# Routed experts on one core: the expert with the fewest tokens takes the last turn

## The chip, the cores and the metric

One NeuronCore of a Trainium2 chip runs the whole program in one launch. The metric is the device time of one execution in microseconds (us); lower is better. Times of the kernel before are the median of three runs; everything about single instructions comes from one profiled execution.

## What is computed

Two layers of a hybrid block over 256 tokens of width 1024. The first layer ends in a dense feed-forward part, the second in eight routed experts, and the change touches the experts alone. Cut to them:

```python
logits = xf @ router                              # [256, 8]
top_val, top_idx = lax.top_k(logits, 2)           # two experts for each token
gates = softmax(top_val)
for e in range(8):                                # over the tokens that chose e
    y_e = (silu(x_e @ w_gate[e]) * (x_e @ w_up[e])) @ w_down[e]
    out[token] += gate * y_e
```

All is float32. An expert has three matrices of 1024 x 3584, 44 MB together. A token can choose any two experts, so the numbers of tokens differ; for this input the experts 0 to 7 have 58, 77, 58, 62, 58, 73, 50 and 76 of them.

## The kernel before

**Order of the work.** The experts come last in the program, after two mixers and the dense feed-forward part. They run one after another, 0 to 7, in `run_experts` (L1714). The weights of an expert are cut into 42 units of 1 MB (`expert_units`, L1376): for each of the chunks in `WIDE` (three of 1024 hidden columns, one of 512) the units of the gate matrix, then those of the up matrix, and one chunk behind them those of the down matrix. All 336 units of the eight experts are one list in the order of their use.

**The feed.** `Feed` (L1398) holds a ring of 18 tiles. The first 18 units are loaded before the experts begin (`load_one`, L1414 is its transfer). After that `send` (L1408 is its transfer) puts the next unit of the list into the ring as soon as the matmuls that read the unit 18 places earlier are done. All these transfers are issued by one engine, SP, in program order, into one queue. `done(k)` in `expert` is k calls of `send`.

**Router.** DVE forms `sel` (which experts a token chose), `pos` (a token's place in its expert, 4096 or more where it didn't choose it) and `gate`. PE sums the counts into `cps`. `count` (L1485) makes `cnt`, then `levi`: 2 for an expert with up to 64 tokens, 1 for up to 96, 0 for more. `gates` (L1353) needs an exponential of ACT and writes `gate`.

**An expert.** `entry(e)` multiplies the first 64 tokens by the 8 units of the first chunk (four of gate, four of up). Then each of PE, ACT, DVE and SP loads `levi[e]` into a register (L1727) and branches (L1787) into one of three versions, the arms of a `tc.Switch`: n = 2, 1 or 0 extra pieces of 32 tokens beyond the first 64. The arm `expert(e, n, ...)` holds the rest: with n > 0 it gathers the extra tokens (`gather(e, 1, AUX)`), adds the results of the expert before to `h` (`scatter`), runs the chunks (`half` for the first 64 tokens, `rest` for the extra ones; `down`, `down_rest`), and the sends of that stretch. Near its end it gathers the next expert's first 64 tokens (`gather(e + 1, 0, ...)`). With n > 0 it closes with `scatter_rest`, or after the last expert with `scatter_last`, followed by the final norm and the output. The hint for the register, the load and the branch of SP stand in front of the sends of the arm.

**Names in the rows.** `mb` and `mc` are PSUM banks (gate and up products; down products, transposes, gathers), `ring` a weight unit, `xT` the gathered tokens, `mh` the hidden values, `ge` the one-hot matrix of a gather, `ys` an expert's result. L97 is the helper for accumulating matmuls, L94 for the others, L100 for transposes.

Of the kernel before, what the change touches and what calls it, by code (L numbers as in the profile page):

```python
# [12 lines left out]
I32 = mybir.dt.int32  # L13
AF = mybir.ActivationFunctionType
OP = mybir.AluOpType
AX = mybir.AxisListType
PSUM = bass.MemoryType.PSUM

P = 128
D = 1024  # L20
# [5 lines left out]
NE = 8  # L26
# [9 lines left out]
def kernel(  # L36
# [37 lines left out]
    nc = tc.nc  # L74
    act = nc.scalar.activation
    vec = nc.vector
# [10 lines left out]
    def mm_bank(name):  # L87
        return pp["mm"].tile([P, 512], F32, tag="mm", name=name)
# [16 lines left out]
    def stream(name, elems, order, side, units, lead, each=None):  # L105
# [6 lines left out]
        def open_raw(stack, once={}, spare=()):  # L112
            pools = [stack.enter_context(tc.tile_pool(name=f"raw{name}{g}", bufs=1, side=side, reuse_waits="tile"))
                     for g in range(n_raw - len(spare))] + list(spare)
            slots.extend([(pools[g], f"raw{g}") for g in order if g not in once])
            for g in order:
                if g in once and units:
                    load_one(*once[g])
                else:
                    load(1 + sum(r[4] for r in raw))  # L120
# [11 lines left out]
        def load(limit=n_raw):  # L132
            while slots and units and sum(r[4] for r in raw) < limit:
                load_one(*slots[0], 1)
                slots.append(slots.pop(0))
# [30 lines left out]
        def get():  # L166
# [3 lines left out]
            return u  # L170

        S.open_raw, S.open_split, S.load_one, S.feed = open_raw, open_split, load_one, units.extend
        S.split, S.ahead, S.get, S.load, S.spl = split, ahead, get, load, spl
        return S
# [93 lines left out]
    iota_f = cst.tile([P, P], F32, name="iota_f")  # L268
# [116 lines left out]
    class Norm:  # L385
        def __init__(self, name):
            self.name, self.ss, self.rstd, self.dg, self.bank = name, {}, {}, {}, None
# [988 lines left out]
    def expert_units():  # L1376
        units = []

        def gate_up(e, c, w):
            for src in (moe_w_gate[0, e], moe_w_up[0, e]):  # L1380
                for k in range(0, KT, 4 // w):
                    units.append((src[k * P:(k + 4 // w) * P, c * 512:(c + w) * 512]
                                  .rearrange("(k p) n -> p k n", p=P), (4 // w, 512 * w)))

        def down(e, c, w):
            for j in range(0, 4 * w, 2):
                r0 = c * 512 + j * P
                units.append((moe_w_down[0, e][r0:r0 + 2 * P, :].rearrange("(p k) n -> p k n", p=P), (2, D)))

        for e in range(NE):  # L1390
            for i, cw in enumerate(WIDE):
                gate_up(e, *cw)
                if i:
                    down(e, *WIDE[i - 1])
            down(e, *WIDE[-1])
        return units

    class Feed:  # L1398
        def __init__(self, units):
            self.units, self.ring, self.sent, self.used = units, [], 0, 0  # L1400

        def view(self, u):
            a, b = self.units[u][1]
            return self.ring[u % len(self.ring)][:, : a * b].rearrange("p (a b) -> p a b", a=a)

        def send(self):
            if self.sent < len(self.units):
                nc.sync.dma_start(self.view(self.sent), self.units[self.sent][0])  # L1408
                self.sent += 1

        def load_one(self, pool, tag):
            self.ring.append(pool.tile([P, 2048], F32, tag=tag, name=f"ring{len(self.ring)}"))
            a, b = self.units[self.sent][1]
            nc.sync.dma_start(self.ring[-1][:, : a * b].rearrange("p (a b) -> p a b", a=a), self.units[self.sent][0])  # L1414
            self.sent += 1

        def get(self, n):
# [6 lines left out]
    def moe(W, R, pend, tidy, prep):  # L1424
# [31 lines left out]
        def make_hn(q, half):  # L1456
            ns = slice(half * 512, (half + 1) * 512)
            vec.scalar_tensor_tensor(hn[:, q, ns], h[:, q, ns], rstd[q], g2b[:, ns], op0=OP.mult, op1=OP.mult)
# [14 lines left out]
        pick(1)  # L1473
        places(lambda: make_hn(1, 0))
        pos = R.t["pos"]
        cnt = R.small("cnt", [P, NE])
        lev = R.small("lev", [P, NE])
        levi = R.small("levi", [P, NE], I32)
        cmax = R.small("cmax", [P, 1])
        cmaxi = R.small("cmaxi", [P, 1], I32)  # L1480
        cps = mm_bank("cps")
# [1 line left out]
            mm(cps[:, :NE], prep[1], R.t["sel"][:, q, :], q == 0, q == 1)  # L1483

        def count():  # L1485
            vec.tensor_copy(cnt, cps[:, :NE])
            vec.tensor_scalar(lev, cnt, 64.5, None, op0=OP.is_lt)
            vec.scalar_tensor_tensor(lev, cnt, 96.5, lev, op0=OP.is_lt, op1=OP.add)
            vec.tensor_copy(levi, lev)
            vec.tensor_reduce(cmax, cnt, axis=AX.X, op=OP.max)  # L1490
            vec.tensor_copy(cmaxi, cmax)

        ge = m2.tile([P, 4, 2, P], F32, name="ge")
# [8 lines left out]
        def onehot(e, base, vs=range(4)):  # L1502
            for v in vs:
                for q in range(2):
                    vec.tensor_scalar(ge[:, v, q, :], slot[:, v, :], float(base), pos[:, q, e:e + 1],  # L1505
                                      op0=OP.add, op1=OP.is_equal)
# [15 lines left out]
        def gather(e, b, bank):  # L1522
            for k in range(KT):
                for q in range(2):
                    mm(bank[:, 64 * k:64 * k + 64], hn[:, q, k * P:(k + 1) * P], ge[:, 0, q, 64 * b:64 * b + 64], q == 0, q == 1)
            act(X[e % 2][:, :, 64 * b:64 * b + 64], bank.rearrange("p (k t) -> p k t", k=KT), AF.Copy)
# [89 lines left out]
        def result():  # L1616
            o = SL, Hid
            ns = [slice(512 * m, 512 * m + 512) for m in range(2)]
            for q in range(2):
                vec.scalar_tensor_tensor(msz[:, q:q + 1], ssz[:, q, 0:1], RMS_EPS, ssz[:, q, 1:2], op0=OP.add, op1=OP.add)  # L1620
                nc.gpsimd.tensor_tensor(rz[:, q:q + 1], msz[:, q:q + 1], mhalf[:, 0:1], op=OP.pow)  # L1621
                vec.tensor_tensor(o[q][1], h[:, q, ns[1]], fg[:, ns[1]], op=OP.mult)
            for q in range(2):
                vec.scalar_tensor_tensor(o[q][0], h[:, q, ns[0]], rz[:, q:q + 1], fg[:, ns[0]], op0=OP.mult, op1=OP.mult)
                act(o[q][1], o[q][1], AF.Copy, scale=rz[:, q:q + 1])
                nc.sync.dma_start(out[0, q * P:(q + 1) * P, ns[0]], o[q][0])
                nc.scalar.dma_start(out[0, q * P:(q + 1) * P, ns[1]], o[q][1])
# [20 lines left out]
        def entry(e):  # L1648
            x = X[e % 2]
            w = WIDE[0][1]  # L1650
            first = []
            for i in range(2):
                first.append(units(2 * w))
                half(GU[i], x, first[i])
                if i == 0:
                    silu(w, 0, 256)
            return first
# [56 lines left out]
        def run_experts(base):  # L1714
            onehot(0, base, range(1))
            if base == 0:
                make_hn(1, 1)
            gather(0, 0, AUX)
            if base == 0:
                count()  # L1720
                gates()
            onehot(0, base, range(1, 4))
            for e in range(NE):
                if base:
                    expert(e, 2, base, entry(e))
                    continue
                lv = nc.values_load(levi[0:1, e:e + 1], engines=ENG, min_val=0, max_val=2)  # L1727
                tc.switch_hint({g: lv for g in ENG}, 3, f"ex{e}")
                first = entry(e)
                at = W.used, W.sent  # L1730
                for arm in tc.Switch({g: lv for g in ENG}, 3, hint=f"ex{e}"):
                    W.used, W.sent = at
                    expert(e, 2 - arm, base, first)
            if base == 0:
                nc.sync.dma_start(fg, final_g.partition_broadcast(P))
            result()

        run_experts(0)
        rv = nc.values_load(cmaxi[0:1, 0:1], min_val=0, max_val=T)
        with tc.If(rv > P):  # L1740
# [15 lines left out]
    W, pend, tidy = mixer(0, Norm("a0"), None, Nf, ffn_weights)  # L1756
# [3 lines left out]
    R = Route()  # L1760
    W, pend, tidy = mixer(1, Na, pend, R, lambda: Feed(expert_units()))
    mst.close()
    moe(W, R, pend, tidy, prep)

_INS = ['x', 'norm1_g', 'w_in', 'pool_w', 'pool_scale', 'conv_w', 'conv_b', 'conv_ln_g', 'conv_ln_b', 'shift_mu', 'rwkv_w0', 'rwkv_w2', 'rwkv_a0', 'rwkv_a2', 'rwkv_g2', 'rwkv_k_k', 'rwkv_k_a', 'rwkv_r_k', 'rwkv_gn_g', 'rwkv_gn_b', 'rwkv_v0', 'rwkv_v1', 'rwkv_v2', 'w_out', 'norm2_g', 'ffn_w_gate', 'ffn_w_up', 'ffn_w_down', 'moe_router', 'moe_w_gate', 'moe_w_up', 'moe_w_down', 'final_g']
# [26 lines left out]
```

## Time and profile before

| what | value |
|---|---|
| median of 3 runs (lowest, highest) | 1427.1 us (1426.35, 1427.16) |
| the profiled execution's own time | 1425.54 us |
| its span, first to last instruction | 1423.6 us |
| PE busy over the span | 1332.7 us, 94% |
| DVE, ACT, POOL busy | 495.4, 296.3, 62.4 us |
| mean granted TensorE clock | 0.991 of full speed |
| read from HBM | 419.86 MB |

The span is 1.9 us less than the profiled execution's time, and that execution is 1.6 us under the median. The experts take the span from about 540 us on. The page cuts the span into 40 slices of 35.6 us each and gives the busy tenths of each engine, the busy share of the 16 DMA engines and the rate that they moved. A share a little over 1 in a window means that all of them were moving data throughout. In a row of the timeline, the bracket at the end names the idle time before the instruction and what ended it.

### The profile page before, as it was taken

What the parts mean: (1) busy time and instruction counts of PE and PEld (TensorE: products, weight loads), DVE (VectorE), ACT (ScalarE), POOL (GpSimd) and SP (SyncE); (2) the same over time, 40 slices, a digit from 0 to 9 for tenths busy, and PEclk for the clock granted to TensorE, in tenths of its full rate; (3) what the DMA queues carried; (4) which work ended last, traced back from release to release, by engine and by line L of the source; (5) the groups of instructions that cost most, each with busy time, mean ns of one, the idle gap of its engine ahead of it and who ended that gap; (6) DMA issues with size and microseconds to landing.
All of it is one profiled execution on the core that took longest, in us unless ns stands there. A gap on an engine that the chain in (4) does not pass through costs nothing.

```text
span 1423.6 us, 32188 instructions
## 1 busy us (share of the span) xinstructions
PE 1332.7 (94%) x14243; PEld 957.1 (67%) x14243; DVE 495.4 (35%) x1065; ACT 296.3 (21%) x524; POOL 62.4 (4%) x89
## 2 busy tenths in 40 slices
PE   8999999999999899999999999888888999999996
PEld 7988799999898877557655555344346665556662
DVE  7999655555698973101010111001001110111001
ACT  6534454444653432000000000000000000000001
POOL 3020220000102010000000000000000000000000
PEclk9999999999999997999999999999999999999998
DMA  5523635551452279999999999999999998999970
GB/s 181 165 74 116 200 129 189 178 180 64 128 162 79 76 284 382 415 416 414 411 418 359 413 416 418 416 415 416 414 417 410 410 413 358 416 415 414 416 280 34
DMA packets 138329, 423.80 MB, mean 298 GB/s; under 512 B 8400, under 2 KB 51800, under 8 KB 123768
## 3 DMA queue, kind: packets, MB, share of 16 engines
q1 hardware_dynamic: 137144, 419.10, 75.7%
q8 instruction: 124, 2.03, 0.6%
q0 software_dynamic: 672, 1.31, 0.3%
q14 instruction: 101, 0.83, 0.2%
q10 hardware_dynamic: 288, 0.52, 0.1%
HBM read 419.86 MB, written 1.05 MB: 296 GB/s over the span
## 4 chain that ended last, share of the span: by engine, by line
PE 70%; DMA 16%; DVE 9%; issue 2%; ACT 1%; POOL 1%; SPq 0%; ACTq 0%; POOLq 0%; DVEq 0%
PE mb L97 26%; PE mc L97 14%; PE fps L94 8%; DMA ring<-in_moe_w_up_dram 7%; DMA ring<-in_moe_w_down_dram 5%; DMA ring<-in_moe_w_gate_dram 4%; PE fd L94 4%; DVE cy L557 3%; PE wo L94 2%; PE pjc L94 2%; PE pjr L94 2%; PE mb L94 2%; PE mc L100 1%; PE mc L94 1%; PE pjp L94 1%
## 5 line engine op out<-in xcount | busy, mean ns | idle before, releaser
L97 PE MATMUL mb<-ring,xT 128*64 128x256 f32 (+1 forms) x6272 | 490.1, 338 | 32.0 <-DMA ring<-in_moe_w_up_dram 13.0
L97 PEld LDWEIGHTS mb<-ring,xT 128*64 128x64 f32 (+1 forms) x6272 | 330.3, 125 | 190.1 <-issue 41.0
L97 PE MATMUL mc<-ring,mh 128*64 128x512 f32 (+1 forms) x1568 | 240.7, 504 | 17.6 <-DMA ring<-in_moe_w_down_dram 9.2
L97 PEld LDWEIGHTS mc<-ring,mh 128*64 128x64 f32 (+1 forms) x1568 | 82.3, 125 | 160.2 <-issue 116.6
L1566 DVE COPY mh<-mc 128x256 f32<-128x256 f32 (+1 forms) x56 | 24.3, 471 | 339.7 <-PE mc L100 339.7
L1551 ACT ACTIVATE sl<-mb 128x256 f32<-128x256 f32 (+2 forms) x62 | 22.9, 398 | 461.9 <-PE mc L100 384.4
L1556 DVE TENSOR_TENSOR sl<-sl,mb 128x256 f32<-128x256 f32 (+1 forms) x56 | 25.1, 469 | 199.0 <-PE mb L97 198.9
L1589 DVE TENSOR_TENSOR h<-h,mc 128x512 f32<-128x512 f32 x34 | 21.5, 683 | 170.5 <-PE mc L97 170.1
L94 PE MATMUL fps<-xhf,wl_fu 128*128 128x256 f32 x176 | 49.9, 284 | 0.1
L94 PE MATMUL fps<-xhf,wh_fg 128*128 128x256 f32 x176 | 49.9, 284 | 0.0
L94 PE MATMUL fps<-xlf,wh_fu 128*128 128x256 f32 x176 | 49.8, 283 | 0.0
L94 PE MATMUL fps<-xhf,wh_fu 128*128 128x256 f32 x176 | 49.8, 283 | 0.0
L94 PE MATMUL fps<-xlf,wh_fg 128*128 128x256 f32 x176 | 49.8, 283 | 0.0
L94 PE MATMUL fps<-xhf,wl_fg 128*128 128x256 f32 x176 | 49.8, 283 | 0.0
L557 DVE SCALAR_TENSOR_TENSOR cy<-cu,parC,cy 128x256 f32<-128x256 f32 x120 | 49.5, 475 | 0.0
L1621 POOL TENSOR_TENSOR rstdz<-msz,mhalf 128x1 f32<-128x1 f32 x2 | 1.6, 830 | 874.3 <-DVE msz L1620 874.3
L151 DVE TENSOR_TENSOR wl_fg<-fg,wh_fg 128x2048 fp32r<-128x2048 f32 x10 | 24.5, 2448 | 30.7 <-ACT wh_fg L147 30.7
L94 PE MATMUL fd<-wh_fd,hh 128*128 128x512 f32 x88 | 34.4, 390 | 0.0
L94 PE MATMUL fd<-wl_fd,hh 128*128 128x512 f32 x88 | 34.4, 390 | 0.0
L94 PE MATMUL fd<-wh_fd,hl 128*128 128x512 f32 x88 | 34.2, 389 | 0.0
L1505 DVE TENSOR_SCALAR ge<-slot,pos 128x128 f32<-128x128 f32 x64 | 14.1, 281 | 57.4 <-PE mc L100 57.3
L94 PEld LDWEIGHTS fps<-xhf,wh_fg 128*128 128x128 f32 x176 | 33.8, 192 | 0.3
(418 smaller groups left out, 2001.1 us busy)
## 6 DMA issues: line engine op xcount, KB each, us to landing
ring<-in_moe_w_gate_dram SPq DMA_DIRECT2D x112, 1024.0 KB
ring<-in_moe_w_up_dram SPq DMA_DIRECT2D x112, 1024.0 KB
ring<-in_moe_w_down_dram SPq DMA_DIRECT2D x112, 1024.0 KB
fg<-in_ffn_w_gate_dram SPq DMA_DIRECT2D x11, 1024.0 KB
fu<-in_ffn_w_up_dram SPq DMA_DIRECT2D x11, 1024.0 KB
fd<-in_ffn_w_down_dram SPq DMA_DIRECT2D x11, 1024.0 KB
wo<-in_w_out_dram SPq DMA_DIRECT2D x16, 512.0 KB
wik<-in_w_in_dram SPq DMA_DIRECT2D x8, 512.0 KB
```

The costliest lines, as they stand in the source:

```text
L94: nc.tensor.matmul(o, lhsT, rhs, start=start, stop=stop)
L97: nc.tensor.matmul(o, lhsT, rhs, start=start, stop=True, skip_group_check=True)
L100: nc.tensor.transpose(o, i, ident[:n, :n])
L151: vec.tensor_tensor(wl[:, :n], t[:, :n], wh.bitcast(F32)[:, :n], op=OP.subtract)
L557: vec.scalar_tensor_tensor(cy[:, i, :], src, wc, cy[:, i, :], op0=OP.mult, op1=OP.add)
L1505: vec.tensor_scalar(ge[:, v, q, :], slot[:, v, :], float(base), pos[:, q, e:e + 1], op0=OP.add, op1=OP.is_equal)
L1551: act(SL[i][:, a:b], GU[0][i][:, a:b], AF.Silu)
L1556: vec.tensor_tensor(SL[i][:, 0:b], SL[i][:, 0:b], GU[1][i][:, 0:b], op=OP.mult)
L1566: vec.tensor_copy(Hid[i][:, 0:b], o[:, 0:b])
L1589: vec.tensor_tensor(h[:, q, ns], h[:, q, ns], ps[n], op=OP.add)
L1621: nc.gpsimd.tensor_tensor(rz[:, q:q + 1], msz[:, q:q + 1], mhalf[:, 0:1], op=OP.pow)
```

## The change

A new function, `least_last`, runs on DVE before the first expert. It finds the expert with the fewest tokens among 1 to 7 and swaps its columns in the counts, in `pos` and in `gate` with those of the eighth place. A second row of `cnt` holds each place's expert number; swapped likewise and cast to integers it is `who`. `levi` is now formed for expert 0 first, and for the other seven after the swap. At the head of each turn but the last SP loads the next turn's expert number from `who` into a register, and the source address of each weight transfer of the turns 1 to 7 is formed from it. For this input the order of the experts becomes 0, 1, 2, 3, 4, 5, 7, 6.

```diff
         def gate_up(e, c, w):
-            for src in (moe_w_gate[0, e], moe_w_up[0, e]):
+            for src in (moe_w_gate, moe_w_up):
                 for k in range(0, KT, 4 // w):
-                    units.append((src[k * P:(k + 4 // w) * P, c * 512:(c + w) * 512]
-                                  .rearrange("(k p) n -> p k n", p=P), (4 // w, 512 * w)))
+                    units.append((lambda x, src=src, k=k: src[0, x, k * P:(k + 4 // w) * P, c * 512:(c + w) * 512]
+                                  .rearrange("(k p) n -> p k n", p=P), (4 // w, 512 * w), e))
...
+            self.index = {}
+
+        def source(self):
+            make, _, e = self.units[self.sent]
+            return make(e) if e == 0 else make(self.index[e])
...
-                nc.sync.dma_start(self.view(self.sent), self.units[self.sent][0])
+                nc.sync.dma_start(self.view(self.sent), self.source())
...
         def count():
-            vec.tensor_copy(cnt, cps[:, :NE])
-            vec.tensor_scalar(lev, cnt, 64.5, None, op0=OP.is_lt)
-            vec.scalar_tensor_tensor(lev, cnt, 96.5, lev, op0=OP.is_lt, op1=OP.add)
-            vec.tensor_copy(levi, lev)
-            vec.tensor_reduce(cmax, cnt, axis=AX.X, op=OP.max)
+            vec.tensor_copy(cnt[:, 0, :], cps[:, :NE])
+            vec.tensor_copy(cnt[:, 1, :], iota_f[:, 0:NE])
+            levels(0, 1)
+
+        def levels(a, b):
+            c = cnt[:, 0, a:b]
+            vec.tensor_scalar(lev[:, a:b], c, 64.5, None, op0=OP.is_lt)
+            vec.scalar_tensor_tensor(lev[:, a:b], c, 96.5, lev[:, a:b], op0=OP.is_lt, op1=OP.add)
+            vec.tensor_copy(levi[:, a:b], lev[:, a:b])
+
+        def least_last():
...
+            vec.scalar_tensor_tensor(score, cnt[:, 0, :], 8.0, cnt[:, 1, :], op0=OP.mult, op1=OP.add)
+            vec.tensor_reduce(least, score[:, ones_], axis=AX.X, op=OP.min)
+            vec.tensor_scalar(took[:, ones_], score[:, ones_], least, None, op0=OP.is_equal)
+            vec.tensor_scalar(kept[:, ones_], took[:, ones_], 0.0, None, op0=OP.is_equal)
...
+            for v in (cnt, pos, R.t["gate"]):
+                w = v[:, :, ones_]
+                x = spare[:, :, ones_]
+                vec.tensor_tensor(x, w, tb, op=OP.mult)
+                vec.tensor_reduce(last, x, axis=AX.X, op=OP.add)
+                vec.tensor_tensor(x, v[:, :, NE - 1:NE].to_broadcast(b3), tb, op=OP.mult)
+                vec.tensor_tensor(w, w, kb, op=OP.mult)
+                vec.tensor_tensor(w, w, x, op=OP.add)
+                vec.tensor_copy(v[:, :, NE - 1], last)
+            levels(1, NE)
+            vec.tensor_copy(who, cnt[:, 1, :])
+            vec.tensor_reduce(cmax, cnt[:, 0, :], axis=AX.X, op=OP.max)
             vec.tensor_copy(cmaxi, cmax)
...
             onehot(0, base, range(1, 4))
+            if base == 0:
+                least_last()
             for e in range(NE):
+                if e + 1 < NE:
+                    W.index[e + 1] = nc.values_load(who[0:1, e + 1:e + 2], engines=(mybir.EngineType.SP,), min_val=1, max_val=NE - 1)
                 if base:
```

How the instructions stand now, at the three places of which the prediction speaks. The first is SP between the last of the 18 preloaded units and the first sends of the first expert. Before:

```order
L1414 DMA ring_6861<-in_moe_w_down_dram 128x2048 [waits DVE_49,DMAHW0_49,PE_49,Activation_49]
L1727 TENSOR_LOAD levi [waits DVE_49]
L1727 ISA x2
L1728 SWITCH_STRIDE
L1728 ISA
L1728 BRANCH_PREFETCH_HINT
L1787 SWITCH_STRIDE
L1787 ISA x2
L1731 BRANCH_PREFETCH_HINT
L1408 DMA ring_5494<-in_moe_w_down_dram 128x2048 [waits DMAHW1_49,PE_49]
```

Now:

```order
L1419 DMA ring_6861<-in_moe_w_down_dram 128x2048 [waits DVE_49,DMAHW0_49,PE_49,Activation_49]
L1761 TENSOR_LOAD who [waits DVE_49]
L1761 ISA x2
L1765 TENSOR_LOAD levi
L1765 ISA x2
L1766 SWITCH_STRIDE
L1766 ISA
L1766 BRANCH_PREFETCH_HINT
L1825 SWITCH_STRIDE
L1825 ISA x2
L1769 BRANCH_PREFETCH_HINT
L1413 DMA ring_5494<-in_moe_w_down_dram 128x2048 [waits DMAHW1_49,PE_49]
```

A load of `who` with a wait for DVE has come ahead of the branch, and every send of the first expert stands behind it.

The second place is DVE from `gate` to its branch. Before:

```order
L1364 TENSOR_TENSOR gate<-ex,zs 128x16 [waits DVE_49]
L1505 TENSOR_SCALAR ge<-slot,pos 128x128 x6
L1727 TENSOR_LOAD levi [waits DVE_49]
L1728 SWITCH_STRIDE
L1728 ISA
```

Now 28 instructions stand between `ge` and the load; the first seven and the last five of them:

```order
L1364 TENSOR_TENSOR gate<-ex,zs 128x16 [waits DVE_49]
L1539 TENSOR_SCALAR ge<-slot,pos 128x128 x6
L1506 SCALAR_TENSOR_TENSOR score<-cnt 128x8
L1507 TENSOR_REDUCE least<-score 128x1 [waits DVE_49]
L1508 TENSOR_SCALAR took<-score,least 128x7 [waits DVE_49]
L1509 TENSOR_SCALAR kept<-took 128x7 [waits DVE_49]
L1516 TENSOR_TENSOR spare<-cnt,took 128x2x7
L1517 TENSOR_REDUCE last<-spare 128x2 [waits DVE_49]
L1518 TENSOR_TENSOR spare<-cnt,took 128x2x7 [waits DVE_49]
```

```order
L1499 SCALAR_TENSOR_TENSOR lev<-cnt,lev 128x7 [waits DVE_49]
L1500 CAST levi<-lev 128x7 [waits DVE_49]
L1523 CAST who<-cnt 128x8
L1524 TENSOR_REDUCE cmax<-cnt 128x1
L1525 CAST cmaxi<-cmax 128x1 [waits DVE_49]
L1765 TENSOR_LOAD levi [waits DVE_49]
```

`who` is the 26th of the 28, behind both the swap of `gate` and the three instructions of `levi`.

The third place is SP among the sends, where the units of the first expert end and those of the second begin. Now:

```order
L1413 DMA ring_6426<-in_moe_w_down_dram 128x2048 [waits DMAHW7_49,PE_49]
L1413 DMA ring_6428<-in_moe_w_down_dram 128x2048 [waits DMAHW0_49,PE_49]
L1413 ISA
L1413 DMA ring_6486<-in_moe_w_gate_dram 128x2x1024 [waits DMAHW1_49,PE_49]
L1413 ISA
L1413 DMA ring_6764<-in_moe_w_gate_dram 128x2x1024 [waits DMAHW2_49,PE_49]
```

From the second expert's units on, one register instruction stands before each transfer; before the change there was none.

## Rows read from the trace of the kernel before

**Rows 1.** The page: GB/s moved by DMA in 40 slices of 35.6 us.

```profile
GB/s 181 165 74 116 200 129 189 178 180 64 128 162 79 76 284 382 415 416 414 411 418 359 413 416 418 416 415 416 414 417 410 410 413 358 416 415 414 416 280 34
```

**Rows 2.** Windows: length, busy of five engines, granted clock, DMA share, GB/s.

```profile
560.00:760.00 200.00, 197.01 (x2311) 122.24 (x2309) 20.40 (x52) 9.86 (x24) 0.00 (x0) 1.00 1.02 413
760.00:768.00 8.00, 5.89 (x37) 2.82 (x38) 2.48 (x4) 0.98 (x2) 0.00 (x0) 1.00 1.00 392
768.00:776.00 8.00, 7.77 (x74) 5.36 (x72) 0.00 (x0) 0.77 (x2) 0.00 (x0) 1.00 0.60 222
...
784.00:1075.00 291.00, 254.48 (x1826) 133.43 (x1824) 30.38 (x83) 12.15 (x30) 0.00 (x0) 1.00 1.02 415
```

**Rows 3.** Timeline of PE: start us, us, instruction; the end of expert 5's `entry`.

```profile
1075.90 1.95 PE L97 MATMUL mb<-ring,xT 128*64 128x256 f32 x16 [0.65 <-DMA ring<-in_moe_w_up_dram]
1077.78 3.79 PE L94 MATMUL mc<-ge,hn 128*128 128x64 f32 x32
```

**Rows 4.** Windows as in rows 2, from expert 6's `entry` to the last `down`.

```profile
1198.00:1407.00 209.00, 205.57 (x2359) 126.90 (x2361) 20.96 (x48) 9.77 (x24) 0.00 (x0) 1.00 0.85 344
...
1270.00:1295.00 25.00, 24.04 (x191) 14.69 (x188) 0.42 (x1) 1.96 (x4) 0.00 (x0) 1.00 1.03 417
```

**Rows 5.** Timeline of DVE where `gate` is made: start us, us, instruction.

```profile
552.77 0.17 DVE L1363 RECIPROCAL zs<-zs 128x2 f32<-128x2 f32 x1
552.97 0.17 DVE L1364 TENSOR_TENSOR gate<-ex,zs 128x16 f32<-128x16 f32 x1
553.06 1.26 DVE L1505 TENSOR_SCALAR ge<-slot,pos 128x128 f32<-128x128 f32 x6
```

**Rows 6.** Timeline of SP: the first two sends of the first expert.

```profile
554.29 2.88 SPq L1408 DMA_DIRECT2D ring<-in_moe_w_down_dram  x2
```

**Rows 7.** SP's register load, branch, arm's first instruction, 540 to 560: ns, start us.

```profile
L1727 SPq TENSOR_LOAD <-levi x1: 468/468/468, 544.3 to 544.3; - x1
...
L1727 SPq SEQ_ASSERT  x1: 28/28/28, 545.1 to 545.1; - x1
...
L1787 SPq COMPARE_BRANCH  x1: 58/58/58, 545.8 to 545.8; - x1
...
L1731 SPq BRANCH_PREFETCH_HINT  x1: 36/36/36, 551.3 to 551.3; - x1
```

**Rows 8.** The same, 760 to 775; the branch into the arm is the second.

```profile
L1787 SPq COMPARE_BRANCH  x2: 43/43/43, 764.0 to 770.4; - x2
...
L1731 SPq BRANCH_PREFETCH_HINT  x1: 36/36/36, 773.0 to 773.0; - x1
```

**Rows 9.** Timeline of PE: the end of expert 5 and `entry` of expert 6.

```profile
1194.90 1.03 PE L97 MATMUL mb<-ys,gT 64*128 64x256 f32 x8
1198.04 14.03 PE L97 MATMUL mb<-ring,xT 128*64 128x256 f32 x128 [2.10 <-DMA ring<-in_moe_w_down_dram]
1212.00 1.99 PE L97 MATMUL mc<-ys,gT 64*128 64x512 f32 x8
```

**Rows 10.** Timeline of PE: expert 2 after its `entry`, to expert 3's.

```profile
782.04 1.99 PE L97 MATMUL mc<-ys,gT 64*128 64x512 f32 x8
...
842.24 3.79 PE L94 MATMUL mb<-ge,hn 128*128 128x64 f32 x32
...
850.30 6.00 PE L97 MATMUL mb<-ring,xT 128*64 128x256 f32 x54
```

**Rows 11.** Timeline of all engines after the last expert's last `down`.

```profile
1407.63 1.14 PE L97 MATMUL mc<-ys,gT 64*128 64x256 f32 x8
1407.74 0.60 ACT L1708 ACTIVATE ys<-mc 128x512 f32<-128x512 f32 x1 [3.15 <-PE mc L97]
...
1409.46 1.02 PE L97 MATMUL mc<-ys,gT 64*128 64x512 f32 x4
...
1410.52 1.29 DVE L1589 TENSOR_TENSOR h<-h,mc 128x512 f32<-128x512 f32 x2 [8.39 <-PE mc L97]
```

**Rows 12.** The chain of waits at expert 7's `entry`: start us, us, what.

```profile
1271.88 21.04 DMA ring<-in_moe_w_up_dram
```

More of the change, by code (lines that the diff above doesn't have):

```diff
@@ L1387, in down @@
                 r0 = c * 512 + j * P
-                units.append((moe_w_down[0, e][r0:r0 + 2 * P, :].rearrange("(p k) n -> p k n", p=P), (2, D)))
+                units.append((lambda x, r0=r0: moe_w_down[0, x, r0:r0 + 2 * P, :].rearrange("(p k) n -> p k n", p=P), (2, D), e))
         for e in range(NE):
@@ L1413, in load_one @@
             a, b = self.units[self.sent][1]
-            nc.sync.dma_start(self.ring[-1][:, : a * b].rearrange("p (a b) -> p a b", a=a), self.units[self.sent][0])
+            nc.sync.dma_start(self.ring[-1][:, : a * b].rearrange("p (a b) -> p a b", a=a), self.source())
             self.sent += 1
@@ L1475, in moe @@
         pos = R.t["pos"]
-        cnt = R.small("cnt", [P, NE])
+        cnt = R.small("cnt")
+        who = R.small("who", [P, NE], I32)
         lev = R.small("lev", [P, NE])
@@ L1485, in count @@
         def count():
-            vec.tensor_copy(cnt, cps[:, :NE])
-            vec.tensor_scalar(lev, cnt, 64.5, None, op0=OP.is_lt)
-            vec.scalar_tensor_tensor(lev, cnt, 96.5, lev, op0=OP.is_lt, op1=OP.add)
-            vec.tensor_copy(levi, lev)
-            vec.tensor_reduce(cmax, cnt, axis=AX.X, op=OP.max)
+            vec.tensor_copy(cnt[:, 0, :], cps[:, :NE])
[7 more added lines that the diff above has]
+        def least_last():
+            score, took, kept = [R.small(n, [P, NE]) for n in ("score", "took", "kept")]
+            least = R.small("least", [P, 1])
+            ones_ = slice(1, NE)
+            vec.scalar_tensor_tensor(score, cnt[:, 0, :], 8.0, cnt[:, 1, :], op0=OP.mult, op1=OP.add)
+            vec.tensor_reduce(least, score[:, ones_], axis=AX.X, op=OP.min)
+            vec.tensor_scalar(took[:, ones_], score[:, ones_], least, None, op0=OP.is_equal)
+            vec.tensor_scalar(kept[:, ones_], took[:, ones_], 0.0, None, op0=OP.is_equal)
+            spare, last = R.small("spare"), R.small("last", [P, 2])
+            b3 = [P, 2, NE - 1]
+            tb, kb = [t[:, None, ones_].to_broadcast(b3) for t in (took, kept)]
+            for v in (cnt, pos, R.t["gate"]):
[10 more added lines that the diff above has]
+            vec.tensor_reduce(cmax, cnt[:, 0, :], axis=AX.X, op=OP.max)
             vec.tensor_copy(cmaxi, cmax)
```

## Prediction

> **What bounds the kernel now.** I read the page's slices first, then windows by stage, then the timelines where one stage hands over to the next. In the slices the transfers run at 410 to 418 GB/s for nearly the whole of the experts, with two lower slices, 359 and 358, and they stop in the last but one [rows 1]. The windows say which side waits. From 784 to 1075 us the DMA share is 1.02 and PE is busy for 254 of 291 us: the transfers bound that stretch [rows 2]. It ends in the `entry` of expert 5, where each unit's 16 matmuls still wait 0.65 us for a transfer; the work on its extra tokens follows at 1077.8 without a wait [rows 3]. From 1198 on PE is the bound: 205.6 of 209 us busy, against a DMA share of 0.85 [rows 4]. So the end of the program has two parts. Up to about 1078 it is as late as the stream of weights; after that it is as late as the sum of PE's work.
>
> Two facts follow. A delay of the stream anywhere before 1075 moves the end, unless a hole in the stream takes it up. And once PE is never idle, the order of the experts changes the end only by what each order adds to or takes from PE's work.
>
> **The swap.** For this input the last turns become expert 7 (76 tokens, one extra piece) and then expert 6 (50 tokens, none). I add PE's time from the start of the seventh turn's `entry`, 1198.04.
> - A turn with one extra piece: the `entry` takes 14.0 us (1198.04 to 1212.00) [rows 9]; from the gather of the extra tokens to the next `entry`, closing included, 120.3 us (1077.78 to 1198.04) [rows 3, 9]. Sum 134.3.
> - A turn without one: `entry` 14.0, the rest 68.3 (782.04 to 850.30), of which 3.8 are the gather for a next expert [rows 10]. As the last turn 14.0 + 68.3 - 3.8 = 78.5.
> - Together 212.8 us. Before, the same stretch took 1407.6 - 1198.0 = 209.6 us [rows 9, 11]. That is 3.2 us more. The price is the closing of an expert with extra tokens: the scattering matmuls and a gap of 2.10 us ahead of the next `entry` [rows 9]. Experts 1 and 5 pay it before; expert 7, being last, has its own closing. Now it pays as well.
> - The end gets shorter. Before, DVE's first addition starts 2.9 us after the last `down` (1407.6 to 1410.5). Without the extra pieces' 16 matmuls there remain ACT's copy, 0.6 us from 0.1 us after the last `down`, and four matmuls of 1.0 us: 1.8 us [rows 11]. That is 1.1 us less.
>
> The swap costs 3.2 - 1.1 = **2.1 us**. I see no gain from having little left to do after the last transfer, since PE arrives there late in either order. The transfers stay ahead in the last turn: 24 units are to be issued after its `entry` begins, 2.53 us each (1.05 MB at 415 GB/s), 61 us, plus a pause of SP of some 9 us at the change of arms [rows 1, 8]. That makes 70 us, and PE needs the last unit about 76 us after the `entry` begins.
>
> **The wait at the start.** This is the larger term. SP now loads `who` ahead of its first branch, and all sends of the first expert stand behind that, though they need no index.
> - DVE: the six instructions on `ge` end at 554.3. `who` is the 26th instruction after them. An instruction that waits for the one before it starts 0.20 us later, one that doesn't 0.09 [rows 5]; 20 of the 26 wait: 20 x 0.20 + 6 x 0.09 = 4.5 us, so `who` is there at about 558.9. All at 0.09 it would be 556.7, all at 0.20 559.5.
> - SP: from a load to the step behind its check 0.8 us; from the load of `levi` to the branch 1.5 us [rows 7]. The branch comes at 558.9 + 0.8 + 1.5 = 561.2.
> - Branch: the arm's first instruction came 5.5 us after it in the first turn, with the transfers at full rate [rows 7], and 2.6 us after it at 770.4, with the transfers at a share of 0.60 [rows 2, 8]. Now the 18 preloaded units have landed before SP gets there, so I take 2.6 and keep 5.5 for the range. The first send then goes out at about 563.9 instead of 554.3 [rows 6]: **9.6 us** later.
>
> [...]
>
> - What takes it up: from 560 to 760 the stream is full, so nothing is regained there [rows 2]. From 760 to 776 it has a hole: 8 x (1.02 - 0.60) + 8 x (1.02 - 1.00) = 3.5 us [rows 2]. It lies where SP, after an expert with extra tokens, sends nothing between its two branches at 764.0 and 770.4 and the fetch behind them [rows 8]. A stream that is 9.6 us late still has data to move then, so the hole fills. PE's lateness in expert 1 would shift the pause too, but the hole is filled as long as that is under 6 us. After it the stream is full to 1075 again. There remain 9.6 - 3.5 = **6.1 us**, and they pass on to the `entry` of expert 5 and to all that follows.
>
> DVE's other work is not late: its next task, the product of the first chunk, waits for PE's `entry` of expert 0, 14.0 us of matmuls at least [rows 9]. PE and ACT load `levi` of expert 0, which is formed earlier as before. The later loads of `who` on SP, seven in all, and the register instruction ahead of 294 transfers cost nothing while the queue is full; at 0.8 us a turn they shorten the 6 us of lead that the transfers keep in the last turn.
>
> **Sum.** 1425.5 for the profiled execution (span 1423.6 and 1.9 around it) + 2.1 + 6.1 = 1433.7. The median of the runs lies 1.6 higher: 1427.1 + 8.2 = **1435.3 us**, slower by 0.6%. About 0.2%, 2.9 us, is what a measurement of this kernel can tell from no change.
>
> **The rivals.**
> - *Faster: PE really waits 21 us at expert 7's `entry`, and the short turn takes that out.* The chain of waits says 21.0 us of DMA there [rows 12]. If PE were idle then, a last turn that needs less PE time would let the end follow the last transfer: 1435.3 - 21 = 1414. It decides if PE's idle time there is more than 11 us. Against it: from 1270 to 1295 PE is busy for 24.0 of 25 us [rows 4]; the chain counts a transfer that ran beside PE's work. Chance 0.05.
> - *No change: the wait for `who` ends in the hole.* That needs a first send no later than 554.3 + 3.5 = 557.8. Then only the swap stays: 1429.2. For it: the first sends feed tiles that PE doesn't need for many us, and I have not seen DVE run these small instructions. Against it: even at 0.09 us each the first send would be at 561.7. Chance 0.13.
> - *Slower still: the fetch behind the branch takes 5.5 us again and the hole does not fill*, because SP's pause there grows as well: 1435.3 + 2.9 + 3.5 = 1441.7. [...] Chance 0.12.
> - *The swap does not take place* (the index stays as it was): 1427.1 + 6.1 = 1433.2. Nothing in the order of the instructions speaks for it. Chance 0.02.
>
> **How the numbers follow.** My forecast has 0.68; its own range, from `who` at 556.7 to a fetch of 5.5 us, is 1433 to 1439. With the no-change case and most of the slower one the range is 1429.0 to 1441.5. Slower by over 0.2%: 0.68 + 0.12 + 0.02 = 0.82; within: 0.13; faster: 0.05.
>
> **What would show it.** In the new profile SP's first send should stand near 564 instead of 554.3, `who` should be cast near 559, and a window around 556 to 564 should show the DMA share near zero. The slice that had 359 GB/s should be full. Expert 5's `entry` should end some 6 us later. The seventh turn should take 134 us on PE and the eighth 78.5 to its last `down`, with no wait for a transfer. I am wrong if expert 5's `entry` ends at the old time, if PE is idle for several us in the last turn, or if the end comes closer to the last transfer without the total moving.

## The result and the profile after

The changed kernel takes 1443.5 us, the median of three runs (1441.87 to 1444.83), against 1427.1. The ratio is 1.012, with a 95% interval of 1.0105 to 1.0134: slower by 16.4 us, where 8.2 were forecast and the range ended at 1441.5. The sign was right and the size forecast was half of what was measured. The profiled execution took 1441.87 us, with a span of 1440.1 and a mean granted clock of 0.991, as before.

The two terms that were forecast came about as forecast. First the start. The timeline of DVE in the changed kernel (start us, us, instruction):

```profile
552.80 0.18 DVE L1364 TENSOR_TENSOR gate<-ex,zs 128x16 f32<-128x16 f32 x1
552.89 1.26 DVE L1539 TENSOR_SCALAR ge<-slot,pos 128x128 f32<-128x128 f32 x6
554.07 0.17 DVE L1506 SCALAR_TENSOR_TENSOR score<-cnt 128x8 f32<-128x8 f32 x1
...
558.60 0.16 DVE L1523 CAST who<-cnt 128x8 int32<-128x8 f32 x1
```

SP's instructions from 554 to 565 us, line by line (ns, and in us the first and the last start):

```profile
L1761 SPq TENSOR_LOAD <-who x1: 474/474/474, 558.8 to 558.8; - x1
...
L1765 SPq TENSOR_LOAD <-levi x1: 275/275/275, 559.6 to 559.6; - x1
...
L1825 SPq COMPARE_BRANCH  x1: 63/63/63, 560.9 to 560.9; - x1
...
L1769 SPq BRANCH_PREFETCH_HINT  x1: 40/40/40, 563.6 to 563.6; - x1
```

And SP's first sends in its timeline:

```profile
563.71 1.18 SPq L1413 DMA_DIRECT2D ring<-in_moe_w_down_dram  x2
```

`who` is cast at 558.6 (forecast 558.9), SP branches at 560.9 (561.2), the arm begins 2.7 us later (2.6) and the first send goes out at 563.71 (563.9), where it stood at 554.29 [rows 6]. The windows of the changed kernel show the pause, and that the hole at 768 to 776 us is gone (columns as in rows 2):

```profile
556.00:564.00 8.00, 8.00 (x78) 5.21 (x76) 2.57 (x19) 0.77 (x2) 0.00 (x0) 1.00 0.02 7
564.00:760.00 196.00, 188.87 (x2209) 115.06 (x2205) 19.84 (x51) 8.60 (x21) 0.00 (x0) 1.00 1.02 406
760.00:768.00 8.00, 7.35 (x69) 4.08 (x68) 0.56 (x1) 0.98 (x2) 0.00 (x0) 1.00 1.03 410
768.00:776.00 8.00, 5.71 (x51) 4.13 (x49) 2.48 (x4) 0.60 (x1) 0.00 (x0) 1.00 1.04 407
784.00:1090.00 306.00, 261.28 (x1860) 135.54 (x1858) 31.11 (x84) 12.13 (x30) 0.00 (x0) 1.00 1.02 406
```

Then the swap. The timeline of PE at the seventh turn's `entry`, at the eighth's (cut off by the window at 1348), and of all engines at the last `down` and behind it:

```profile
1213.09 14.04 PE L97 MATMUL mb<-ring,xT 128*64 128x256 f32 x128 [2.27 <-issue]
...
1346.02 2.34 PE L97 MATMUL mb<-ring,xT 128*64 128x256 f32 x19 [1.21 <-DMA ring<-in_moe_w_down_dram]
...
1421.20 3.65 PE L97 MATMUL mc<-ring,mh 128*64 128x512 f32 x16 [0.52 <-DVE mh L1600]
...
1424.96 0.60 ACT L1742 ACTIVATE ys<-mc 128x512 f32<-128x512 f32 x1 [15.00 <-PE mc L97]
...
1426.77 1.28 DVE L1623 TENSOR_TENSOR h<-h,mc 128x512 f32<-128x512 f32 x2 [5.62 <-PE mc L97]
```

The seventh turn takes 132.9 us (134.3 forecast). The eighth takes 78.8 to the end of its last `down` (78.5), at 1424.85, 0.1 us ahead of ACT's copy. DVE's first addition follows 1.9 us behind it (1.8). From the seventh `entry` to the end of the span it is now 227.0 us, against 1423.6 - 1198.04 = 225.6 before [rows 9]. The swap therefore costs 1.4 us in these two executions, where the forecast was 2.1.

What was not forecast stands in the last column of the windows. At the same DMA share of 1.02 the stream moves 406 GB/s where it moved 413 and 415 [rows 2]. The slices of the page say the same, 398 to 412 in full ones where 410 to 418 stood [rows 1]:

```profile
GB/s 190 166 61 140 173 139 192 188 176 75 114 150 75 113 293 292 406 410 409 404 412 407 404 410 402 407 410 401 407 411 398 407 409 343 272 408 380 343 407 173
```

So the stream arrives much later at the place where it last decides. This is the end of expert 5's `entry` in the timeline of PE, which answers to rows 3:

```profile
1091.05 1.95 PE L97 MATMUL mb<-ring,xT 128*64 128x256 f32 x16 [0.65 <-DMA ring<-in_moe_w_up_dram]
1092.93 3.79 PE L94 MATMUL mc<-ge,hn 128*128 128x64 f32 x32
```

It was 1077.78 and is 1092.93: 15.15 us later instead of 6.1. The rest, 16.5 - 15.15 = 1.4 us of the span, is the swap.

### The profile page after: what moved, and what is told of

It reads as the page before. It is cut to its first block, busy times and chain, and to the rows that moved or that the text cites. A ratio compares the mean times of both kernels' runs of the same rounds, so it can differ in the third digit from the quotient of the medians.

```text
span 1440.1 us, 32831 instructions
## 1 busy us (share of the span) xinstructions
PE 1333.3 (93%) x14243; PEld 955.6 (66%) x14243; DVE 502.0 (35%) x1096; ACT 296.2 (21%) x524; POOL 62.8 (4%) x89
## 4 chain that ended last, share of the span: by engine, by line
PE 66%; DMA 20%; DVE 10%; issue 2%; ACT 1%; POOL 1%; SPq 0%; ACTq 0%; DVEq 0%; POOLq 0%
PE mb L97 25%; PE mc L97 13%; PE fps L94 8%; DMA ring<-in_moe_w_up_dram 8%; DMA ring<-in_moe_w_down_dram 7%; PE fd L94 4%; DMA ring<-in_moe_w_gate_dram 3%; DVE cy L557 3%; PE mb L94 2%; PE pjk L94 2%; PE pjr L94 2%; PE pjc L94 1%; PE mc L100 1%; PE mc L94 1%; PE wo L94 1%
```

## The experiments

**What the theories are.** The DMA engines were busy throughout in both kernels (a share of 1.02) and moved less, so each packet (one of the pieces in which the trace lists a transfer, here of 2048, 4096 or 8192 bytes) takes longer. From 640 to 1100 us the trace has a median of 162 ns for the packets of 4096 bytes in the changed kernel and 159 before; for 2048 bytes it is 87 and 84, for 8192 bytes 313 and 309. Three or four nanoseconds come on top whatever the size. The transfers of the first expert, whose addresses are still constants, show it too: its 4096-byte packets have a median of 162 ns where they had 159, its 2048-byte packets 87 where they had 84.

*Theory A* looks at where the packets go. The new small tiles (`who`, `score`, `took`, `kept`, `least`, `spare`, `last` and a second row of `cnt`) lie in the same pool as the old ones, and whatever is allocated behind that pool moves up by 288 bytes a partition. Among it are ring tiles 7 to 15. In the compiled programs they lie at:

```
                   ring 7, 8, ... 15 (bytes)         above a multiple of 256
before             32256, 40448, ... 97792           0
after              32544, 40736, ... 98080           32
ring 0 to 6, 16, 17, both kernels                    224
```

Theory A is that this move is what costs: a packet into a tile that begins off a multiple of 256 bytes takes three to four nanoseconds longer, whatever its size. It names no mechanism, and no run shows one. That 256 is the size that counts is an assumption of mine at this point; runs 2, 7 and 8 move the tiles by 288, 64 and 256 bytes. *Rival B* is that the addresses read from a register, or SP's extra instruction ahead of each transfer, slow the stream. The runs are compared by their ratio to the kernel before on the same chip, and by a distance within one profile: from the start of the first `entry` to the extra tokens of expert 5, 527.2 us before and 542.5 after the change. The first `entry` in PE's timeline, before and after:

```profile
550.57 15.72 PE L97 MATMUL mb<-ring,xT 128*64 128x256 f32 x120 [0.69 <-ACT xT L1526]
...
550.40 15.83 PE L97 MATMUL mb<-ring,xT 128*64 128x256 f32 x132 [0.69 <-ACT xT L1560]
```

**1. The ring put back, the rest of the change kept.**

```diff
-            spare, last = R.small("spare"), R.small("last", [P, 2])
+            spare, last = R.small("spare", [P, 2, NE + 28]), R.small("last", [P, 2])
...
-                x = spare[:, :, ones_]
+                x = spare[:, :, 1:NE]
```

> The changed kernel with one tile, `spare`, made 224 bytes a partition larger, so that ring tiles 7 to 15 lie again at the place within 512 bytes that they had before the change (32256, 40448 and so on, which are multiples of 512, instead of 32544, 40736, each 32 bytes past a multiple of 256). Nothing else differs. Theory A (the new small tiles moved half of the ring, and each packet into a moved tile takes 3 to 4 ns longer): the median of the 4096-byte packets goes back from 162 to 159 ns, the rate from 404 to 409 GB/s back to 412 to 417, the `entry` of expert 5 ends near 1084 instead of 1093, and the time is 1435 us (1433.5 to 1436.5). Rival B (the addresses read from a register, or SP's extra instruction ahead of each transfer, slow the stream): nothing moves, 1443.5 us (1442 to 1445), packets as in the changed kernel. Rival C (the rate differs from build to build for a reason that has nothing to do with either): packets at neither value, and a time that fits neither.

Measured: 1435.1 us, ratio 1.0066 (1.0053 to 1.0079). The windows and PE's timeline at the end of expert 5's `entry`:

```profile
564.00:760.00 196.00, 190.10 (x2220) 117.01 (x2216) 19.84 (x51) 8.61 (x21) 0.00 (x0) 1.00 1.02 413
784.00:1075.00 291.00, 254.20 (x1812) 132.52 (x1810) 31.12 (x84) 12.14 (x30) 0.00 (x0) 1.00 1.02 413
```

```profile
1082.29 1.95 PE L97 MATMUL mb<-ring,xT 128*64 128x256 f32 x16 [0.65 <-DMA ring<-in_moe_w_up_dram]
1084.17 3.79 PE L94 MATMUL mc<-ge,hn 128*128 128x64 f32 x32
```

The rate is 413 instead of 406, the medians are 84, 159 and 309 ns again, and expert 5's extra tokens come at 1084.2, 534.4 us after the first `entry`. 224 bytes of padding take back 1.0120 - 1.0066 = 0.0054, or 7.7 us. Rival B, which expected no change, falls. It also puts the kernel where the forecast had put it: 8.2 us on 1427.1 are a ratio of 1.0057, within the interval.

**2. The ring moved, nothing else changed.**

```diff
-        lev = R.small("lev", [P, NE])
+        lev = R.small("lev", [P, NE + 72])[:, 0:NE]
```

> The kernel before with `lev` made 288 bytes a partition larger, of which the first 32 are used as before: ring tiles 7 to 15 then lie where the changed kernel has them within 512 bytes. No instruction is added. Theory A: 4096-byte packets at a median of 162 ns instead of 159, 404 to 409 GB/s in the full stretches; some 9 to 10 us of extra transfer time up to the `entry` of expert 5 (217 units of 0.045 us), of which the hole at 760 to 776 us takes 3.5; the end comes 5 to 6.5 us later, 1432 to 1433.5 us. Rival B (register addresses): this kernel has none, so it stays at 1427.1 (1426 to 1428).

Measured: 1436.8 us, ratio 1.0075 (1.0062 to 1.0088), 3 us above the expected band. The windows show the rate of theory A, in a kernel without one register address:

```profile
564.00:760.00 196.00, 193.12 (x2271) 119.48 (x2269) 20.40 (x52) 9.59 (x23) 0.00 (x0) 1.00 1.02 408
784.00:1075.00 291.00, 249.90 (x1774) 128.94 (x1768) 29.79 (x82) 12.04 (x30) 0.00 (x0) 1.00 1.02 409
```

At 408 instead of 415 GB/s a unit of 1.0486 MB takes 0.043 us longer. About 200 units are sent up to expert 5's `entry` (5 x 42 + 8, less the 18 preloaded), 8.7 us, and its extra tokens come 8.0 us later (535.2 for 527.2). The hole at 760 to 784 us took much less than the 3.5 us that I had set against it: the rate there rises only from 335 to 353 GB/s. The remaining 3 us lie at the end. One part, 1.3 us, is expert 7's `entry`, which in this order follows the short turn of expert 6; three units are now late by 0.53 to 0.62 us each, where one was by 0.44 before. PE's timeline there:

```profile
1299.44 1.95 PE L97 MATMUL mb<-ring,xT 128*64 128x256 f32 x16 [0.53 <-DMA ring<-in_moe_w_up_dram]
1302.01 1.95 PE L97 MATMUL mb<-ring,xT 128*64 128x256 f32 x16 [0.62 <-DMA ring<-in_moe_w_up_dram]
1304.55 1.95 PE L97 MATMUL mb<-ring,xT 128*64 128x256 f32 x16 [0.59 <-DMA ring<-in_moe_w_up_dram]
```

The other part, 1.7 us, is a fall of the clock in the profiled execution, told in the last section. That the rate fell by the same amount in two programs and came back in a third, each time with the place, leaves nothing for rival C of run 1 (a rate that differs from build to build).

**3. No wait at the start.** Expert 1 is no candidate for the last turn here, and its address is a constant.

```diff
-            return make(e) if e == 0 else make(self.index[e])
+            return make(e) if e < 2 else make(self.index[e])
...
-            ones_ = slice(1, NE)
+            ones_ = slice(2, NE)
...
-                if e + 1 < NE:
+                if 0 < e < NE - 1:
```

> The changed kernel with the candidates cut to experts 2 to 7 and the address of expert 1 a constant, so that SP's first turn loads no index: it sends the first expert's refills without waiting for DVE's 26 small instructions. The swap (expert 6 for 7) and the place of the ring stay as in the changed kernel. Theory A with the start's wait as one separate term of 9.4 us that nothing takes up, since the slower packets have already filled the hole at 760 to 776: first send near 554.5 instead of 563.7, the `entry` of expert 5 ends 5 to 6 us later than before (1083 to 1084), 1433.5 us (1432.5 to 1435). Rival D (the start's wait is mostly swallowed on the way, and something else makes the change slow): the time stays above 1438. Rival B would have the transfers of the first two experts, whose addresses are constants here, at the old 159 ns a 4096-byte packet; theory A has them at 162.

Measured: 1437.0 us, ratio 1.0080 (1.0067 to 1.0092). The first send goes out at 553.27 (some 554.5 expected), and expert 5's extra tokens come at 1084.74 (1083 to 1084 expected). The total is 2 us above the expected band, in which I had let the slower packets fill the hole at 760 to 784 us (334 GB/s there, 335 before: it took up nothing). The first two experts' packets, with constant addresses, are at 162 ns a 4096-byte packet, so rival B falls once more. Rival D wanted a time above 1438; the median is below that, but the interval reaches to 1439, so the time alone does not decide. The trace does: with the place of the ring unchanged, the wait at the start is worth 542.5 - 535.1 = 7.4 us up to expert 5; by the totals (1.0120 - 1.0080 = 0.0040) it is 5.7 us.

**4. The swap alone, by constants in the kernel before.**

```diff
+    TURNS = (0, 1, 2, 3, 4, 5, 7, 6)
...
-        for e in range(NE):
+        for e in TURNS:
...
-                lv = nc.values_load(levi[0:1, e:e + 1], engines=ENG, min_val=0, max_val=2)
+                lv = nc.values_load(levi[0:1, TURNS[e]:TURNS[e] + 1], engines=ENG, min_val=0, max_val=2)
```

(`pos` and `gate` are indexed by `TURNS[e]` likewise.)

> The kernel before with the experts' turns written as constants in the order 0 1 2 3 4 5 7 6: the swap that the change makes for this input, with no instruction on DVE or SP for it and no tile moved. The swap's term measured by itself. By the two traces the stretch from the seventh turn's `entry` to the end grows from 225.6 to 227.0 us: 1428.6 us (1427.8 to 1429.4), with the `entry` of expert 5 at its old 1077.8. The prediction's sum for it was 2.1 us: 1429.2. Rival (the short last turn lets the end follow the last transfer, so the swap alone is a gain): below 1426.

Measured: 1427.9 us, ratio 1.0013 (1.0004 to 1.0022): a loss of 1.9 us, 0.6 to 3.1. Expert 5's extra tokens come after 527.2 us, exactly as before. The short last turn gains nothing.

**5. Both remedies, swap kept.** Runs 1 and 3 together; the padding is that of run 1.

> Both remedies together: the changed kernel with the ring's tiles back at multiples of 512 bytes and with no load of the index in SP's first turn (candidates 2 to 7). What is left of the change: the swap, DVE's small instructions, and the transfers of experts 2 to 7 whose address comes from a register. If the place of the ring, the wait at the start and the swap are all of it: as the swap by constants, 1427.9 us (1427 to 1429), rate 412 to 416 GB/s, and the `entry` of expert 5 followed by its extra tokens near 1078. Rival (the register addressing costs something of its own, however little): 1430 or more, and the extra tokens of expert 5 later than 1080.

Measured: 1431.5 us, ratio 1.0029 (1.0018 to 1.0039), over the expected band and where the rival had it (1430 or more). Up to expert 5 it is not as the rival had it: 415 GB/s, 527.8 us after the first `entry`, extra tokens at 1079.3 (the rival: later than 1080). The profiled execution lost time elsewhere: its first `entry` began 1.0 us later than that of the kernel before, and the clock fell once in the last turn, which cost 1.7 us (last section). That is less than half of the 6.5 us between the profiled executions of runs 5 and 4. It left open whether the register addressing has a small price of its own; run 9 asks for it.

**6. All 18 tiles at multiples of 512, in the kernel before.**

```diff
     res = ctx.enter_context(tc.tile_pool(name="res", bufs=1))
+    rpad = ctx.enter_context(tc.tile_pool(name="rpad", bufs=1, side="right"))
+    nc.gpsimd.memset(rpad.tile([P, 120], F32, name="rpadt"), 0.0)
```

> The kernel before with one unused tile of 480 bytes a partition at the top of the right side, so that ring tiles 0 to 6, 16 and 17, which lie at 480 above a multiple of 512, lie at multiples of 512 too; all 18 are then aligned. Theory A says that these nine tiles have paid the same 3 to 4 ns a packet all along: the 2048-byte packets of 88 ns go, the mean of the 4096-byte packets falls from 161.5 towards 159 ns, the rate rises from 415 to about 421 GB/s. Some 135 units after the hole at 760 to 784 us gain 0.045 us each, 6 us; what is gained ahead of the hole only makes it longer. 1420 us (1417 to 1422). Rival E (only tiles whose place is not a multiple of some smaller size than these have pay, or the cost lies in the move as such): 1426 as before.

Measured: 1422.5 us, ratio 0.9972 (0.9961 to 0.9983), 3.4 us under the kernel before by the medians, 4.0 by the ratio, and the fastest of all that ran, just outside the expected 1417 to 1422. The windows and the page's slices:

```profile
760.00:784.00 24.00, 21.87 (x195) 14.57 (x197) 2.48 (x4) 1.75 (x4) 0.00 (x0) 1.00 0.81 303
784.00:1075.00 291.00, 256.04 (x1836) 134.19 (x1834) 31.10 (x84) 12.13 (x30) 0.00 (x0) 1.00 1.02 420
```

```profile
GB/s 183 165 74 117 199 125 193 178 179 63 131 149 91 77 249 379 417 422 419 417 421 338 416 420 419 420 420 421 419 420 417 417 417 358 419 421 418 418 270 34
```

The mean of the 2048-byte packets falls from 86.2 to 84.1 ns and the rate rises from 415 to 420. As expected, what is gained ahead of 760 us only deepens the hole (303 GB/s for 335). The gain is 3.4 to 4 us rather than 6, since from 415 to 420 GB/s only 0.03 us a unit come off and not 0.045 (135 units, 4 us). The nine tiles at 224 above a multiple of 256 had thus been paying in the kernel before.

**7 and 8. How fine the place matters.** `lev` is enlarged as in run 2, by 64 and by 256 bytes instead of 288.

```diff
+        lev = R.small("lev", [P, NE + 16])[:, 0:NE]
```

> The kernel before with ring tiles 7 to 15 moved by 64 bytes (64 above a multiple of 512, where the shift of 288 put them 32 above a multiple of 256). It tells how fine the place matters. If any place that is no multiple of 256 costs the 3 to 4 ns: as the shift by 288, 1436.8 us (1435 to 1438), 408 GB/s. If only a place that is no multiple of 64 does: 1426 us, 415 GB/s. [...]

> The kernel before with ring tiles 7 to 15 moved by 256 bytes. The control of the shifts by 64 and 288: a move as large, to a multiple of 256 that is none of 512. If multiples of 256 are enough: 1426 us (1425 to 1428), 415 GB/s, 4096-byte packets at a median of 159 ns. If it takes a multiple of 512, or if any move of the layout costs: 1432 to 1438 us and 408 GB/s.

Measured: with 64 bytes 1437.0 us, ratio 1.0078 (1.0064 to 1.0091); with 256 bytes 1426.3 us, ratio 1.0003 (0.9994 to 1.0012). The window from 784 to 1075 us of the first and of the second:

```profile
784.00:1075.00 291.00, 251.61 (x1784) 130.06 (x1780) 31.10 (x84) 11.36 (x28) 0.00 (x0) 1.00 1.02 409
```

```profile
784.00:1075.00 291.00, 254.64 (x1826) 133.57 (x1824) 30.79 (x84) 12.13 (x30) 0.00 (x0) 1.00 1.02 415
```

A move as such costs nothing. A place 64 above a multiple of 256 costs what 32 above costs, and a multiple of 256 that is none of 512 is free. So of the offsets that ran, 32, 64 and 224 above a multiple of 256 cost (runs 2, 7 and 6), and a whole multiple of 256 does not (run 8). Others, 128 among them, were not tried.

**9. The register addressing alone.** The indices are the plain numbers, formed early; there is no choice of the least expert and no swap, and ring tiles 7 to 15 lie at multiples of 256, as good as before the change.

```diff
-            levels(0, 1)
+            levels(0, NE)
+            vec.tensor_copy(who, iota_f[:, 0:NE])
...
-            if base == 0:
-                least_last()
```

(`cmax` and `cmaxi` follow in `count` as before the change; `lev` has 192 bytes of padding.)

> What is left to be told apart: the run with both remedies came to a ratio of 1.0029 to the kernel before, the swap by constants to 1.0013; the intervals overlap. Here the changed kernel without DVE's choice of the least expert: the indices are the plain numbers 0 to 7, formed next to `levi` and so there as early, and the experts run in their old order; addresses of experts 1 to 7 still come from a register, SP still loads one before each turn, and the ring's tiles 7 to 15 lie at multiples of 256 bytes. If the register addressing and SP's loads cost nothing by themselves: 1426 us (1425 to 1427.5), rate 415 GB/s, first send at most 1 us later than 554.3, extra tokens of expert 5 within 1 us of 527.2 us after the first `entry`. If they are what the run with both remedies had over the swap: 1428 to 1429.5 us.

Measured: 1425.0 us, ratio 0.9991 (0.9981 to 1.0000); 527.1 us from the first `entry` to expert 5's extra tokens, first send at 554.87. Addresses from a register, seven loads on SP and the extra instruction ahead of 294 transfers cost nothing that this measurement can tell. What run 5 lost over run 4 is not theirs; the two intervals overlap. Run 5's executions had the lower clock, which would explain most of it (last section).

**10. The change with all 18 tiles in place.** The paddings of runs 1 and 6 together.

> The changed kernel, wait at the start and swap included, with all 18 ring tiles at multiples of 512 bytes (the enlarged `spare` and the unused 480 bytes on the right side together). If the terms add up: ratio of the changed kernel 1.012, less 0.0054 for the nine tiles that the change moved, less 0.0028 for the nine others, 1.0038: 1431 us (1429.5 to 1432.5); extra tokens of expert 5 some 530 to 531 us after the first `entry`, against 534.4 with only the first nine in place. If it comes out under 1427, the wait at the start is hidden once the stream is fast enough, and the place was the whole matter; if over 1433.5, the gain by the other nine tiles is there only while nothing delays the stream.

Measured: 1430.3 us, ratio 1.0027 (1.0016 to 1.0038), 529.0 us to expert 5's extra tokens (530 to 531 expected). The time lies in the expected band: the terms add up. Even with a faster stream, the change is slower than the kernel before, and 8 us slower than run 6.

## Why the prediction was half right

**The swap (forecast +2.1).** Right: +1.9 by run 4, +1.4 in the two profiles. The rival that saw 21 us of waiting at expert 7's `entry` is answered by run 4, which takes the short turn last and is no faster. The chain of waits had named a transfer that ran beside PE's work.

**The wait at the start (forecast 9.6 us at the first send, 6.1 at the end).** Right in its parts: 9.4 us at the first send. In the profiles 7.2 us are left of it up to expert 5 by run 1 (534.4 - 527.2), and 7.4 by run 3 against the changed kernel. By the totals it is 7.6 us by run 1 less run 4 (1.0066 - 1.0013 = 0.0053), 5.7 by the changed kernel less run 3, and 5.3 by run 1 less run 5 (1.0066 - 1.0029 = 0.0037), so 6.1 lies among them. Up to expert 5 the hole gave back some 2 us and not 3.5. It was full in run 1 as it is after the change, but run 1's stream ran at 413 GB/s behind it where 415 stood before, which over 291 us is another 1.4 us; why it did was not traced. The branch instruction itself took 63 ns, against 43 and 58 before [rows 7, 8], and nothing hangs on it, since the arm came 2.7 us behind it. The prediction calls that time a fetch. The trace has packets of an instruction queue in it (one of 8192 bytes at 549.7 us before, three at 561.3 to 562.3 now), but not for which engine; that a fetch takes up the time is not shown.

**The step that failed** is the last of the prediction's sentences on the stream, "After it the stream is full to 1075 again", from which followed that 6.1 us remain and pass on. It was full, at a share of 1.02. But a full share is not a rate: 1.02 went with 415 GB/s before and with 406 after. The sum had no term for what the new small tiles do to the places of all tiles behind them. That term measures 7.7 us (changed kernel less run 1), 10.7 us in the kernel before alone (run 2). The forecast of 8.2 plus the 7.7 is 15.9; 16.4 was measured. The new tiles stand in the change's code, and the addresses in the built program could have been read before it ran.

**The rivals.** The case "slower still" had nearly the right number, 1441.7, by mechanisms that did not occur: the arm came 2.7 us behind the branch, not 5.5, and the hole filled. That is a coincidence. "No change" fell with the first send at 563.7. "The swap does not take place" fell with the turns' lengths. "Faster" is answered by run 4. A rival for the place was missing. By the units as they were measured afterwards it would have been worth 200 x 0.04 to 0.05 us, 8 to 10 us, and the range would have ended near 1451.

## What to carry to other kernels

Where a stretch is bound by a stream of transfers, look at GB/s beside the DMA share, and read from the built program where its destinations lie; a small tile in a pool ahead of them moves those that lie behind it, and nothing in the diff's instructions shows it. Here 64 bytes of padding a partition cost 11 us in the wrong place (run 7), and 480 gained 4 in the right one (run 6). A decision that is formed late should be loaded behind the work that does not need it: here 4.5 us of small instructions and a branch held up sends that had no use for the index.

## What the runs showed that was not expected

**The place of a destination.** With all 18 tiles off a multiple of 256 (by 32, 64 and 224 bytes) packets take 3 to 4 ns longer than with none off, at 2048, 4096 and 8192 bytes alike (means of 88.2, 164.0 and 317.3 ns in the changed kernel, 84.1, 160.1 and 314.1 in run 6). From 784 to 1075 us the stream runs at 406 to 409 GB/s with nine tiles off by 32 or 64 and nine by 224, at 413 to 415 with nine off by 224 alone, at 418 to 420 with none.

It is not a fixed price of each packet. The packets carry no tile's name, but their sizes and order tell the unit, and so the tile. Right behind the pause at the start of the changed kernel, the 4096-byte packets into ring tile 2 (571.8 to 574.3 us) have the fast median of 159 ns, and those into tile 4 (from 576.8) 164, though both tiles lie at 224. And of the packets into ring tile 16, which lies at 224 in both kernels, 3% were slow (more than 1 ns over the fast value) in a typical round of the ring in the kernel before, where tiles 7 to 15 ahead of it lie at multiples of 256, and 83% after the change. The price sets in some units behind the first tile that is off. What delays it was not traced.

**A fall of the clock at the change of turns.** In some executions the granted clock goes to 0.50 for 3.4 us just after an `entry` begins that follows about 2 us of idle PE. PE's timeline and the windows of run 5 at its eighth `entry`:

```profile
1331.30 1.03 PE L97 MATMUL mb<-ys,gT 64*128 64x256 f32 x8
1334.52 15.72 PE L97 MATMUL mb<-ring,xT 128*64 128x256 f32 x128 [2.19 <-DMA ring<-in_moe_w_down_dram]
```

```profile
1330.30:1334.50 4.20, 2.03 (x18) 1.47 (x17) 2.48 (x4) 0.60 (x1) 0.00 (x0) 1.00 0.92 299
1334.70:1338.10 3.40, 3.40 (x18) 2.44 (x17) 0.00 (x0) 0.00 (x0) 0.00 (x0) 0.50 0.59 241
1338.10:1345.00 6.90, 6.90 (x66) 5.49 (x64) 0.00 (x0) 0.77 (x2) 0.00 (x0) 1.00 0.64 222
```

The `entry` takes 15.7 us instead of 14.0, so one fall costs 1.7 us. The profiled executions of runs 1, 2, 5, 7 and 8 have it at one or two such gaps; those of the kernel before, of the change and of runs 3, 4, 6, 9 and 10 at none, with gaps as long (2.10 us [rows 9], 2.50 in run 3). What decides was not found. It goes with the spread between executions of one kernel: of 60 executions of the kernel before, 12 had a mean granted clock of 0.991 and took 1424.9 us on average, 32 had 0.990 and 1426.1, 12 had 0.989 and 1427.8. One fall of 3.4 us takes 0.0012 off the mean clock. Run 5's executions have 0.9890 on average and run 4's 0.9904; at the 1.2 to 1.7 us that 0.001 goes with, this is some 2 of the 2.5 us between the means of the two runs, an estimate from these numbers.
